# All four branch merges at the end of a layer, every gate in seven products

## The chip, the cores and the metric
The kernel runs on one core of a Trainium2 chip. Its time is device time in microseconds; of three runs the median is 1343.72 (1343.64 to 1344.62). A profile of one more execution shows what each engine did: TensorE (PE) multiplies matrices into PSUM, VectorE (DVE) and ScalarE (ACT) work element by element, GpSimd (POOL) raises a few numbers to a power, SyncE (SP) issues transfers.

## What is computed
A trunk of two layers on 512 tokens of width 1024, all in float32. A layer normalises its input, projects it with one wide matrix, runs four token mixers of width 512 (A, a gated linear recurrence; B, a state space model; C, an mLSTM; D, retention) and merges them:

```
hn = rmsnorm(x, norm_g);  proj = hn @ w_in          # 1024 x 12304: inputs of the mixers, then 4 x 1024 gates
y_a, y_b, y_c, y_d = ...                            # each 512 x 512, with its own output gate
up = einsum('bsnw,nwd->bsnd', [y_a, y_b, y_c, y_d], w_branch)
g = sigmoid(gates)                                  # 512 x 4 x 1024
x = x + sum_n(g * up) @ w_out
```

## The kernel before
Each float32 operand is split into a high and a low part, and a product is made of three matmuls, high by high, high by low and low by high (`mm3`, lines 330 to 333). The weights are in a list of pieces, `PLAN`, of 128 x 1024 numbers each, in the order of use. SP fetches them one after the other into three raw buffers (`wr`); ScalarE makes the high part (`wh`), VectorE the low one (`wl`), four buffers of each. Five pieces are asked for ahead of use.

TensorE follows the projections in the order in which `layer` calls them. `proj_T` and `proj_W` give outputs of 512 columns: 96 matmuls of 128x512 for a projection to 512 columns. In `proj_W` four accumulators of tokens (`pm`) are filled in turn, 6 matmuls each, over four pieces of weights.

A merge has four blocks of 256 gate columns. In merges A and B a block is a `proj_T` of the gates (48 matmuls of 512 columns) and one of the branch output (24). In merges C and D the gates of a block are computed by `seven`: gates and tokens are halved, rows of the weight too, and of the eight products of quarters seven are left, with sums of quarters as operands (Strassen's scheme in Winograd's form). It has 7 x 4 x 3 = 84 matmuls of 256 columns, and the same 24. The sums of activations (T1 to T4) are made once a layer by `combine`; T3 is written over a quarter of the normalised input by `in_place`, so that no projection can follow. The sums of weights are made for each block by `split7` on VectorE.

The mixers are generators (`branch_a` to `branch_d`, `finish_cd`) in a list of jobs. Behind pieces of a projection `pump(us)` hands the first job a credit of time, and the job puts its next instructions into the program until the credit is used up; the rate given to `start` scales it (a higher rate, more steps for the same credit). `drain` puts all that is left of a job there at once. A scheduler then orders each engine's instructions by priority; the evacuation of an accumulator and the weights go first. An engine runs its instructions in that order.

The order of a layer is: v of C, inputs of A and B, output gate of B, q and k of C, output gate of A; merge A; merge B, with C's mixer as a job at rate 0.4; q and k of D (one projection), v of D; o and z of C with D's mixer as a job and `combine` beside; z of D, with C's finish as a job; merge C, with D's finish; merge D; the output projection.

The lines that matter later: the splits of a branch output for a merge (yh, yl, lines 948 and 949), the rotary embedding of D's q and k (lines 1066 to 1070), C's exponents, scores and scaled keys (EC line 1255, PC line 1264, ke line 1270), B's last steps (xd, line 1238) with the transposes of `finish` (lines 401 and 860).

Of the kernel before, what the change touches and what calls it, by code (L numbers as in the profile page):

```python
# [10 lines left out]
AF = mybir.ActivationFunctionType  # L11
ALU = mybir.AluOpType
# [5 lines left out]
P = 128  # L18
NT = S // P
# [24 lines left out]

SEVEN = (2, 3)


def plan():  # L50
    u = []

    def proj(name, b, w=256):
        for h in range(2):
            u.append(("in", OFF[name] + 256 * b, h))

    def merge(n):
        for b in range(4):
            if n in SEVEN:
                for h in range(2):  # L60
                    u.append(("in7", OFF["g"] + 256 * (4 * n + b), h))
            else:
                proj("g", 4 * n + b)
            u.append(("br", n, 256 * b))

    def wide(*names):
        for name in names:
            for q in range(4):
                u.append(("in4", OFF[name], q))

    for name, b in BLOCKS:
        if b is None:
            wide(name)
        else:
            proj(name, b)
    merge(0)
    merge(1)

    wide("dq", "dv", "co", "cz", "dz")
    merge(2)  # L80
    merge(3)
    for q in range(4):
        u.append(("out4", 0, q))
    for b in range(2, 4):
        for h in range(2):
            u.append(("out", 256 * b, h))
    return u
# [10 lines left out]
D_DM, D_DS, D_COS, D_SIN, D_N = 0, 512, 768, 1024, 1280  # L98
# [6 lines left out]
def body(ctx, tc, x_in, wu, wz, ag, pp, br, fg, cst, cstd, out, xs, rows):  # L105
# [20 lines left out]
    def heap(name, shape=(P, 512), dt=F32):  # L126
        return hp.tile(list(shape), dt, name=nm(name), tag="h", bufs=NH)
# [4 lines left out]
    def tmain(name, shape=(P, 512), dt=F32):  # L132
        return hp.tile(list(shape), dt, name=nm(name), tag="tm", bufs=NTM)
# [186 lines left out]
    def drain(job):  # L320
        while any(j[0] is job for j in jobs):
            for _ in jobs[0][0]:
                pass
            jobs.pop(0)

    def start(job, rate):
        jobs.append((job, rate))
        return job
# [38 lines left out]
    def proj_W(acts, consume):  # L367

        ps = [psm() for _ in range(NT)]
        for q in range(4):  # L370
            hi, lo = take(1)[0]
            for t in range(NT):
                s = slice(t * P, (t + 1) * P)
                for i in range(2):
                    j = 2 * q + i
                    o = slice(512 * i, 512 * i + 512)
                    mm3(ps[t], acts[j][0][:, s], acts[j][1][:, s], hi[:, o], lo[:, o], j == 0, j == 7)
                if q == 3:
                    with tc.high_priority():
                        consume(t, ps[t])  # L380
                if t % 2:
                    pump(2.6)
# [39 lines left out]
    def gate2(dst, z):  # L422

        A.activation(dst, z, AF.Tanh, scale=0.5)
        V.scalar_tensor_tensor(dst, dst, 1.0, z, ALU.add, ALU.mult)
# [388 lines left out]
    def layer(l, hn, hn2, first=None):  # L814
        p, b = prm[l], brd[l]
# [83 lines left out]
        def quarter(r, s):  # L899
            return [[hn2[j][:, 4 * r + k, 256 * s:256 * s + 256] for k in range(4)] for j in range(2)]  # L900
# [30 lines left out]
        def in_place():  # L931
# [5 lines left out]
                    V.tensor_tensor(hn2[1][o], t3[kk], hn2[0].bitcast(F32)[o], ALU.subtract)  # L937
            bq["T3"] = quarter(0, 1)


        md = [None] * KT
        mp = [None] * KT

        def merge(n, y):
            yT = []
            for k in range(4):
                h, q = pair("y")
                A.copy(h, y[k])
                V.tensor_tensor(q, y[k], h.bitcast(F32), ALU.subtract)
                yT.append((h, q))  # L950
            tail = None
            if n == SEVEN[0]:
                in_place()
            for blk in range(4):
                th = [None, None]

                def use_g(ct, ps):
                    th[ct] = tmain("tg")
                    A.activation(th[ct], ps, AF.Tanh, scale=0.5)

                def use_up(ct, ps, blk=blk, th=th):
                    k = 2 * blk + ct
                    if n == 0:
                        md[k] = heap("md")
                        V.scalar_tensor_tensor(md[k], th[ct], 1.0, ps, ALU.add, ALU.mult)
                        return
                    V.scalar_tensor_tensor(th[ct], th[ct], 1.0, ps, ALU.add, ALU.mult)
                    V.tensor_tensor(md[k], md[k], th[ct], ALU.add)
                    if n == 3:
                        mp[k] = pair("mp")  # L970
                        A.activation(mp[k][0], md[k], AF.Copy, scale=0.5)
                        V.scalar_tensor_tensor(mp[k][1], md[k], 0.5, mp[k][0].bitcast(F32),
                                               ALU.mult, ALU.subtract)

                if n not in SEVEN:
                    proj_T(hn, use_g)
                    proj_T(yT, use_up, 1)
                    continue
                tail = seven(th, tail, yT, use_up)
            if n in SEVEN:  # L980
                tail()
# [4 lines left out]
        def seven(th, tail, yT, use_up):  # L986
# [58 lines left out]
                pump(2.6)  # L1045
            return rest

        merge(0, yA)

        drain(jB)  # L1050
        hC = []
        jC = start(branch_c(l, qT, kT, v1, am, fcs, em, hC), 0.4)

        merge(1, yB)


        qk = [None] * NT
        cos = cd[:, D_COS:D_COS + 256].rearrange("p (j t i) -> p j t i", j=2, t=NT)
        sin = cd[:, D_SIN:D_SIN + 256].rearrange("p (j t i) -> p j t i", j=2, t=NT)

        def use_qk(t, ps):

            r = heap("qk", [P, 8, 2, 32])
            u, v = tmain("ropeu", [P, 8, 2, 32]), tmain("ropev", [P, 8, 2, 32])
            for w, f in ((u, cos), (v, sin)):
                V.tensor_tensor(w.rearrange("p (j h) e i -> p j (h e) i", j=2),
                                ps.rearrange("p (j h i) -> p j h i", j=2, i=32),
                                f[:, :, t, :].unsqueeze(2).to_broadcast([P, 2, 8, 32]), ALU.mult)
            V.tensor_tensor(r[:, :, 0, :], u[:, :, 0, :], v[:, :, 1, :], ALU.subtract)
            V.tensor_tensor(r[:, :, 1, :], v[:, :, 0, :], u[:, :, 1, :], ALU.add)  # L1070
            qk[t] = r

        proj_W(hn, use_qk)
        vD = [heap("vD") for _ in range(NT)]
        proj_W(hn, lambda t, ps: A.copy(vD[t], ps))
        drain(jC)
        yDr = []
        jD = start(branch_d(qk, vD, yDr), 0.35)


        steps = combine()
        bq.update(B11=quarter(0, 0), B21=quarter(1, 0), B22=quarter(1, 1))
        tC = [heap("tC") for _ in range(NT)]

        def use_o(t, ps):
            A.activation(tC[t], ps, AF.Tanh, scale=0.5)
            V.scalar_tensor_tensor(hC[t], tC[t], 1.0, hC[t], ALU.add, ALU.mult)

        proj_W(hn, use_o)
        for _ in range(4):  # L1090
            next(steps, None)
        proj_W(hn, lambda t, ps: gate2(tC[t], ps))
        for _ in steps:
            pass

        def finish_cd(y, z, yT, mul, gcol):
            for j in range(4):
                yT[j] = heap("yC")
            for q in range(2):
                for t in (2 * q, 2 * q + 1):  # L1100
                    head_norm(y[t], z[t], mul)
                    yield 1.2
                if q:
                    for t in range(2):
                        finish(y[t], t, yT, gcol)
                    yield 2.4
            yield 1.2
            for t in range(2, NT):
                finish(y[t], t, yT, gcol)
            yield 2.4  # L1110

        drain(jD)
        yC = [None] * 4
        jF = start(finish_cd(hC, tC, yC, 0.25 / P, 44), 1.0)


        tD = [heap("tD") for _ in range(NT)]
        proj_W(hn, lambda t, ps: gate2(tD[t], ps))
        drain(jF)
        yD = [None] * 4  # L1120
        jG = start(finish_cd(yDr, tD, yD, 1.0 / P, 48), 0.5)
        merge(2, yC)
        drain(jG)
        merge(3, yD)
# [6 lines left out]
    def head_norm(y, z, mul):  # L1131

        sq = tran("sq")
        A.activation(sq, y, AF.Square)
        ss = small("hs", [P, 4])
        V.tensor_reduce(ss, sq.rearrange("p (h d) -> p h d", d=P), AX.X, ALU.add)
        r = small("hr", [P, 4])
        rsqrt(r, ss, mul, 4)
        y3 = y.rearrange("p (h d) -> p h d", d=P)
        V.tensor_tensor(y3, y3, bc(r, P), ALU.mult)  # L1140
        V.tensor_tensor(y, y, z, ALU.mult)
# [411 lines left out]
```

## Time and profile before
| | |
|---|---|
| median of three runs | 1343.72 us |
| profiled execution, its time | 1343.94 us |
| its span, first to last instruction | 1342.1 us |
| PE, DVE, ACT busy | 1327.7, 875.9, 578.5 us |
| merge A, B, C, D of layer 1 | 76.1, 80.9, 65.1, 63.4 us |
| granted TensorE clock, mean | 0.999 |

A row of the timeline gives an instruction's start and length in us. A matmul's end is modelled and overlaps the next one's start, so the distance of starts is its price, not its length. A row of the windows gives the length of a stage, and for each engine the busy time and number of instructions in it. A stage begins with its first projection matmul.

### The profile page before, as it was taken

How to read it: one execution, taken by the hardware profiler on the slowest of the kernel's cores; microseconds unless marked ns; L12 is line 12 of the kernel's file. 1: busy time of each engine (PE TensorE's matmuls, PEld its weight loads, DVE VectorE, ACT ScalarE, POOL GpSimd, SP SyncE). 2: the span in 40 equal slices, each digit the busy share in tenths (PEclk: the TensorE clock that was granted, in tenths of full speed). 3: DMA queues.
4: the chain of work that ended last, by engine and by line, in shares of the span. 5: the costliest groups of instructions: out<-in, count | busy, mean ns of one | idle time of the engine just before them, and what ended most of it. 6: DMA issues, size and time to landing. Idle time of an engine off the chain costs nothing.

```text
span 1342.1 us, 18162 instructions
## 1 busy us (share of the span) xinstructions
PE 1327.7 (99%) x7180; PEld 1123.7 (84%) x7180; DVE 875.9 (65%) x1504; ACT 578.5 (43%) x968; POOL 29.9 (2%) x53
## 2 busy tenths in 40 slices
PE   9999999999999999999999999999999999999998
PEld 8877888888888889998897778888888888899987
DVE  6668778444543798686466696873455448887845
ACT  6387334322213465454443963352222135554533
POOL 1000000000000020000000000000000000100000
PEclk9999999999999999999999999999999999999999
DMA  6223332333233223335332333333323322233351
GB/s 233 92 79 94 110 111 80 111 93 92 69 90 95 63 74 88 107 95 188 128 98 84 97 101 117 110 95 94 94 63 93 96 79 63 64 95 95 96 187 63
DMA packets 42181, 133.48 MB, mean 99 GB/s; under 512 B 5336, under 2 KB 5592, under 8 KB 42096
## 3 DMA queue, kind: packets, MB, share of 16 engines
q1 hardware_dynamic: 39504, 128.06, 30.9%
q10 hardware_dynamic: 2592, 4.27, 0.9%
q8 instruction: 56, 0.92, 0.3%
q14 instruction: 29, 0.24, 0.1%
HBM read 128.06 MB, written 4.24 MB: 99 GB/s over the span
## 4 chain that ended last, share of the span: by engine, by line
PE 84%; DVE 7%; ACT 6%; issue 2%; POOL 1%; DMA 0%; POOLq 0%; ACTq 0%; DVEq 0%
PE pm L331 23%; PE pm L332 23%; PE pm L333 23%; PE px L331 2%; PE px L333 2%; PE px L332 2%; PE px L1209 1%; ACT wh L278 1%; DVE wl L288 1%; PE pm L534 1%; PE px L401 1%; PE px L1282 1%; PE px L1262 1%; PE px L1362 1%; DVE cv L632 0%
## 5 line engine op out<-in xcount | busy, mean ns | idle before, releaser
L288 DVE TENSOR_TENSOR wl<-wr,wh 128x1024 fp32r<-128x1024 f32 (+1 forms) x184 | 225.1, 1224 | 240.3 <-ACT wh L278 239.4
L278 ACT CAST wh<-wr 128x1024 fp32r<-128x1024 f32 (+1 forms) x184 | 192.9, 1049 | 331.8 <-PE pm L332 170.1
L331 PE MATMUL pm<-hn,wh 128*128 128x512 f32 (+1 forms) x768 | 291.2, 379 | 0.0
L333 PE MATMUL pm<-hn,wl 128*128 128x512 f32 (+1 forms) x768 | 289.6, 377 | 0.0
L332 PE MATMUL pm<-hn,wh 128*128 128x512 f32 (+1 forms) x768 | 289.4, 377 | 0.0
L331 PE MATMUL pm<-wh,hn 128*128 128x512 f32 (+2 forms) x480 | 181.2, 378 | 1.3 <-DVE cv L632 1.3
L332 PE MATMUL pm<-wl,hn 128*128 128x512 f32 (+2 forms) x480 | 179.2, 373 | 0.0
L333 PE MATMUL pm<-wh,hn 128*128 128x512 f32 (+2 forms) x480 | 178.8, 373 | 0.0
L331 PEld LDWEIGHTS pm<-hn,wh 128*128 128x128 f32 x768 | 144.6, 188 | 30.3 <-issue 2.2
L332 PEld LDWEIGHTS pm<-hn,wh 128*128 128x128 f32 x768 | 144.5, 188 | 28.3 <-issue 0.4
L333 PEld LDWEIGHTS pm<-hn,wl 128*128 128x128 f32 x768 | 144.6, 188 | 27.8
L331 PEld LDWEIGHTS pm<-wh,hn 128*128 128x128 f32 x480 | 90.3, 188 | 19.5 <-ACT th L850 1.1
L333 PEld LDWEIGHTS pm<-wh,hn 128*128 128x128 f32 x480 | 90.3, 188 | 17.0
L332 PEld LDWEIGHTS pm<-wl,hn 128*128 128x128 f32 x480 | 90.4, 188 | 16.3 <-DVE wl L288 0.2
L331 PE MATMUL pm<-yh,wh 128*128 128x512 f32 x256 | 101.0, 397 | 0.0
L332 PE MATMUL pm<-yl,wh 128*128 128x512 f32 x256 | 100.7, 394 | 0.0
L333 PE MATMUL pm<-yh,wl 128*128 128x512 f32 x256 | 100.6, 394 | 0.0
L252 ACT CAST wh<-wr 128x1024 fp32r<-128x1024 f32 x48 | 50.4, 1050 | 54.1 <-DVE wr L263 43.6
L255 DVE TENSOR_TENSOR wl<-wr,wh 128x1024 fp32r<-128x1024 f32 x48 | 58.7, 1224 | 11.0 <-ACT wh L252 11.0
L332 PE MATMUL pm<-wl,mph 128*128 128x256 f32 (+1 forms) x192 | 61.4, 320 | 0.0
L331 PE MATMUL pm<-wh,mph 128*128 128x256 f32 (+1 forms) x192 | 61.3, 319 | 0.0
L333 PE MATMUL pm<-wh,mpl 128*128 128x256 f32 (+1 forms) x192 | 61.3, 319 | 0.0
(336 smaller groups left out, 2089.3 us busy)
## 6 DMA issues: line engine op xcount, KB each, us to landing
wr<-in_wu_dram SPq DMA_DIRECT2D x212, 512.0 KB, 3.6
row<-rows SPq DMA_DIRECT2D x24, 256.0 KB, 4.3
x<-in_x_dram SPq DMA_DIRECT2D x15, 256.0 KB, 5.3
wr<-in_wz_dram SPq DMA_DIRECT2D x4, 544.0 KB, 5.1
xs<-x ACTq DMA_DIRECT2D x8, 256.0 KB, 2.9
x<-xs SPq DMA_DIRECT2D x8, 256.0 KB, 6.4
out_dram<-xo SPq DMA_DIRECT2D x4, 256.0 KB, 2.1
out_dram<-xo ACTq DMA_DIRECT2D x4, 256.0 KB, 2.4
```

The source lines that it names most:

```text
L252: A.copy(w[0], s)
L255: V.tensor_tensor(w[1], s, w[0].bitcast(F32), ALU.subtract)
L278: h = A.copy(hi, raw)
L288: d = V.tensor_tensor(lo, raw, hi.bitcast(F32), ALU.subtract)
L331: mm(ps, lh, rh, start=first, stop=False, **kw)
L332: mm(ps, lh, rl, start=False, stop=False, **kw)
L333: lastpm[0] = mm(ps, ll, rh, start=False, stop=last, **kw)
L401: nc.tensor.transpose(ps[:, j * P:(j + 1) * P], src[:, j * P:(j + 1) * P], ident)
L534: pin(mm(bank[t][:, :272], xn[t, h][:, j * P:(j + 1) * P], ws.raw[h][:, 272 * j:272 * j + 272], start=h == 0 and j == 0, stop=h == 1 and j ...
L1209: mm(two(py, t)[:, 64 * e:64 * e + 64], M[e][:, t, :], xdt[t][:, o:o + 64], start=True, stop=True)
L1262: mm(ps[:, t], kT[h][:, s], qT[h][:, s], start=True, stop=True)
L1282: mm(pi[:, i], Ps[h][:, t], v1[t][:, h], start=True, stop=True)
```

## The change
All four gates are computed in seven products, and the four merges stand together at the end of the layer. q, k and v of D, o and z of C and z of D come ahead of merge A. C's mixer becomes a job before q and k of D, at rate 0.65 (was 0.4), behind what is left of B's mixer. The finishes of C and D both become jobs at the start of merge A, at rate 0.3 (were 1.0 and 0.5). The pieces of weights are listed in the new order; the projections, mixers and their numbers of instructions stay as they are.

```diff
-SEVEN = (2, 3)
+SEVEN = (0, 1, 2, 3)
...
-    merge(0)
-    merge(1)
 
     wide("dq", "dv", "co", "cz", "dz")
-    merge(2)
-    merge(3)
+    for n in range(4):
+        merge(n)
...
+        hC = []
+        jC = start(branch_c(l, qT, kT, v1, am, fcs, em, hC), 0.65)
...
+        proj_W(hn, use_qk)
+        vD = [heap("vD") for _ in range(NT)]
+        proj_W(hn, lambda t, ps: A.copy(vD[t], ps))
+        drain(jC)
+        yDr = []
+        jD = start(branch_d(qk, vD, yDr), 0.35)
...
+        proj_W(hn, use_o)
+        for _ in range(4):
+            next(steps, None)
+        proj_W(hn, lambda t, ps: gate2(tC[t], ps))
...
+        drain(jD)
...
+        tD = [heap("tD") for _ in range(NT)]
+        proj_W(hn, lambda t, ps: gate2(tD[t], ps))
...
+        yC, yD = [None] * 4, [None] * 4
+        jF = start(finish_cd(hC, tC, yC, 0.25 / P, 44), 0.3)
+        jG = start(finish_cd(yDr, tD, yD, 1.0 / P, 48), 0.3)
         merge(0, yA)
-
         drain(jB)
-        hC = []
-        jC = start(branch_c(l, qT, kT, v1, am, fcs, em, hC), 0.4)
-
         merge(1, yB)
...
         drain(jF)
-        yD = [None] * 4
-        jG = start(finish_cd(yDr, tD, yD, 1.0 / P, 48), 0.5)
         merge(2, yC)
         drain(jG)
         merge(3, yD)
```

On TensorE, in the projection to q and k of D, layer 1 (accumulators pm_3151 to pm_3154 before, pm_2086 to pm_2089 now; in the changed kernel the three matmuls of `mm3` are lines 329 to 331, the rotary embedding 951 to 955, C's mixer begins at 1250, the splits of y are at 1011), the order before held nothing else:

```order
L331 MATMUL pm_3153<-wh_3022,hn_120 128x512
L332 MATMUL pm_3153<-wl_3023,hn_120 128x512
L333 MATMUL pm_3153<-wh_3022,hn_121 128x512
L331 MATMUL pm_3153<-wh_3022,hn_120 128x512
L332 MATMUL pm_3153<-wl_3023,hn_120 128x512
L333 MATMUL pm_3153<-wh_3022,hn_121 128x512
L331 MATMUL pm_3154<-wh_3022,hn_120 128x512
```

In the changed kernel the same place has the last transposes of B's output (xd) and the first scores (qT, kT) and key transposes of C:

```order
L399 MATMUL px_2077<-cst_sb,xd_1590 128x128 x4
L399 MATMUL px_2120<-cst_sb,xd_1599 128x128 x4
L331 MATMUL pm_2088<-wh_1819,hn_121 128x512
L399 MATMUL px_2129<-cst_sb,xd_1608 128x128 x4
L1257 MATMUL px_2148<-qT_1387,kT_1543 128x128 x4
L1263 MATMUL px_2155<-cst_sb,kT_1543 128x128 x3
L329 MATMUL pm_2088<-wh_1819,hn_120 128x512
L330 MATMUL pm_2088<-wl_1820,hn_120 128x512
L331 MATMUL pm_2088<-wh_1819,hn_121 128x512
L329 MATMUL pm_2089<-wh_1819,hn_120 128x512
L330 MATMUL pm_2089<-wl_1820,hn_120 128x512
L331 MATMUL pm_2089<-wh_1819,hn_121 128x512
```

The last 60 small matmuls of B's mixer and the first 28 of C's now stand between the 96 of this projection; the 96 others of C's mixer stand in the projection to v of D behind it.

On VectorE, the rotary embedding of D's q and k (ropeu and ropev from the accumulators, then qk) stood before with only weight splits (wl) among it:

```order
L288 TENSOR_TENSOR wl_3218<-wr_3215,wh_3217 128x1024
L1066 TENSOR_TENSOR ropeu_3258<-pm_3151,cstd_sb 128x512
L1066 TENSOR_TENSOR ropev_3259<-pm_3151,cstd_sb 128x512
L1066 TENSOR_TENSOR ropeu_3271<-pm_3152,cstd_sb 128x512
L1066 TENSOR_TENSOR ropev_3272<-pm_3152,cstd_sb 128x512
L1066 TENSOR_TENSOR ropeu_3284<-pm_3153,cstd_sb 128x512
L1069 TENSOR_TENSOR qk_3257<-ropeu_3258,ropev_3259 128x8x32
L1069 TENSOR_TENSOR qk_3270<-ropeu_3271,ropev_3272 128x8x32
L1070 TENSOR_TENSOR qk_3257<-ropev_3259,ropeu_3258 128x8x32
L1070 TENSOR_TENSOR qk_3270<-ropev_3272,ropeu_3271 128x8x32
L288 TENSOR_TENSOR wl_3248<-wr_3245,wh_3247 128x1024
```

Now it has C's scores (PC), scaled keys (ke) and exponents (EC) among it:

```order
L954 TENSOR_TENSOR qk_2275<-ropeu_2276,ropev_2277 128x8x32
L954 TENSOR_TENSOR qk_2288<-ropeu_2289,ropev_2290 128x8x32
L955 TENSOR_TENSOR qk_2275<-ropev_2277,ropeu_2276 128x8x32
L951 TENSOR_TENSOR ropeu_2321<-pm_2088,cstd_sb 128x512
L951 TENSOR_TENSOR ropev_2322<-pm_2088,cstd_sb 128x512
L951 TENSOR_TENSOR ropeu_2334<-pm_2089,cstd_sb 128x512
L955 TENSOR_TENSOR qk_2288<-ropev_2290,ropeu_2289 128x8x32
L286 TENSOR_TENSOR wl_2266<-wr_2263,wh_2265 128x1024
L951 TENSOR_TENSOR ropev_2335<-pm_2089,cstd_sb 128x512
L1250 SCALAR_TENSOR_TENSOR EC_2295<-row_2247,am_646,cst_sb 128x128 x2
L1259 TENSOR_TENSOR PC_2306<-px_2301,EC_2295 128x512
L1265 TENSOR_TENSOR ke_2312<-px_2308,EC_2295 128x384
```

The product of the last scores, PC_2306, and ke_2312 stand behind all four accumulators' rotary products; C's first matmuls with v in the next projection need them.

On VectorE, at the start of merge D before (yl is the low part of a branch output, tg a half gate, md the merged sum, wal and wl weight splits of a block in seven products):

```order
L968 TENSOR_TENSOR md_2205<-md_2205,tg_4153 128x512
L949 TENSOR_TENSOR yl_4830<-yC_4168,yh_4829 128x512
L967 SCALAR_TENSOR_TENSOR tg_4154<-tg_4154,pm_4387 128x512
L255 TENSOR_TENSOR wal_4334<-wr_4280,wah_4333 128x512
L288 TENSOR_TENSOR wl_4150<-wr_4147,wh_4149 128x1024
L968 TENSOR_TENSOR md_2220<-md_2220,tg_4154 128x512
L1013 TENSOR_TENSOR tg_4353<-tg_4353,pm_4415 128x256
L949 TENSOR_TENSOR yl_4834<-yC_4169,yh_4833 128x512
L949 TENSOR_TENSOR yl_4838<-yC_4170,yh_4837 128x512
L949 TENSOR_TENSOR yl_4842<-yC_4171,yh_4841 128x512
```

And at the start of merge B now:

```order
L1011 TENSOR_TENSOR yl_3964<-yB_1962,yh_3963 128x512
L253 TENSOR_TENSOR wal_3988<-wr_3903,wah_3987 128x512
L1011 TENSOR_TENSOR yl_3968<-yB_1963,yh_3967 128x512
L1011 TENSOR_TENSOR yl_3972<-yB_1964,yh_3971 128x512
L1011 TENSOR_TENSOR yl_3976<-yB_1965,yh_3975 128x512
L1075 TENSOR_TENSOR tg_4007<-tg_4007,pm_4054 128x256
L1011 TENSOR_TENSOR yl_4626<-yC_3244,yh_4625 128x512
L1011 TENSOR_TENSOR yl_4630<-yC_3245,yh_4629 128x512
L1081 TENSOR_TENSOR tg_4008<-tg_4008,px_4009 128x256
L1011 TENSOR_TENSOR yl_4634<-yC_3246,yh_4633 128x512
L253 TENSOR_TENSOR wl_3982<-wr_3979,wh_3981 128x1024
L1011 TENSOR_TENSOR yl_4638<-yC_3247,yh_4637 128x512
```

Behind B's four splits those of C's output follow in the same block, and further on those of D's; before, each merge had its own four at its start.

## Rows read from the trace of the kernel before
**Rows 1.** The page: busy time by engine; chain of waits by engine.
```profile
PE 1327.7 (99%) x7180; PEld 1123.7 (84%) x7180; DVE 875.9 (65%) x1504; ACT 578.5 (43%) x968; POOL 29.9 (2%) x53
...
PE 84%; DVE 7%; ACT 6%; issue 2%; POOL 1%; DMA 0%; POOLq 0%; ACTq 0%; DVEq 0%
```

**Rows 2.** What PE waited for, first two of six: us in total, times, longest.
```profile
PE px L401 <- DVE xn L450: 2.1, 4, 0.6
PE px L401 <- DVE xd L1238: 1.7, 4, 0.6
```

**Rows 3.** Windows of layer 1: length; busy us (count) of PE, PEld, DVE, ACT, POOL; clock; DMA.
```profile
136.00:158.40 22.40, 22.40 (x97) 18.02 (x96) 20.85 (x28) 7.40 (x10) 0.00 (x0) 1.00 0.26 76
213.80:289.90 76.10, 75.24 (x349) 61.38 (x348) 38.17 (x72) 28.50 (x54) 2.59 (x4) 1.00 0.34 104
289.90:370.80 80.90, 80.90 (x414) 68.03 (x413) 43.52 (x77) 19.83 (x27) 0.00 (x0) 1.00 0.26 79
370.80:393.10 22.30, 22.30 (x98) 18.09 (x97) 9.29 (x12) 4.14 (x4) 0.00 (x0) 1.00 0.33 94
...
...
497.60:562.70 65.10, 64.89 (x450) 59.88 (x449) 51.76 (x74) 35.73 (x70) 0.00 (x0) 1.00 0.30 85
562.70:626.10 63.40, 63.33 (x433) 58.16 (x432) 47.13 (x67) 29.86 (x49) 0.00 (x0) 1.00 0.40 122
```

**Rows 4.** Windows of merges A to D, layer 2, same columns.
```profile
877.60:953.80 76.20, 75.36 (x350) 61.47 (x350) 38.16 (x72) 28.52 (x54) 2.58 (x4) 1.00 0.34 104
953.80:1034.60 80.80, 80.80 (x413) 67.99 (x412) 43.52 (x77) 19.72 (x26) 0.00 (x0) 1.00 0.27 79
1161.50:1227.30 65.80, 64.97 (x449) 59.94 (x448) 52.48 (x75) 35.65 (x69) 0.00 (x0) 1.00 0.30 89
1227.30:1290.80 63.50, 63.41 (x434) 58.10 (x433) 47.27 (x67) 29.98 (x50) 0.00 (x0) 1.00 0.40 122
```

**Rows 5.** Timeline of PE in merge D: start, length, instruction.
```profile
608.68 0.28 PE L332 MATMUL px<-hn,wah 128*128 128x256 f32 x1
608.80 0.28 PE L333 MATMUL px<-hn,wal 128*128 128x256 f32 x1
608.92 0.39 PE L331 MATMUL pm<-yh,wh 128*128 128x512 f32 x1
609.15 0.39 PE L332 MATMUL pm<-yl,wh 128*128 128x512 f32 x1
```

**Rows 6.** Timeline of DVE, merge A's surroundings and the rotary embedding.
```profile
203.78 1.23 DVE L288 TENSOR_TENSOR wl<-wr,wh 128x1024 fp32r<-128x1024 f32 x1
204.92 1.65 DVE L1185 TENSOR_SCALAR E<-row,am 128x128 f32<-128x128 f32 x8
...
230.32 1.13 DVE L1255 SCALAR_TENSOR_TENSOR EC<-row,am,cst_sb 128x128 f32<-128x128 f32 x4
...
389.92 0.68 DVE L1066 TENSOR_TENSOR ropeu<-pm,cstd_sb 128x512 f32<-128x512 f32 x1
390.52 0.68 DVE L1066 TENSOR_TENSOR ropev<-pm,cstd_sb 128x512 f32<-128x512 f32 x1
...
392.91 0.75 DVE L1069 TENSOR_TENSOR qk<-ropeu,ropev 128x256 f32<-128x256 f32 x2
```

**Rows 7.** Lines of DVE in merge B and after: count, busy us, mean ns.
```profile
L1264 DVE TENSOR_TENSOR PC<-px,EC 128x512 f32<-128x512 f32 x4 | 2.7, 687 | 6.0 <-PE px L1262 6.0
...
L949 DVE TENSOR_TENSOR yl<-yB,yh 128x512 fp32r<-128x512 f32 x4 | 2.5, 684 | 0.0
...
L1270 DVE TENSOR_TENSOR ke<-px,EC 128x384 f32<-128x384 f32 x4 | 2.2, 546 | 0.0
```

**Rows 8.** Timeline of ACT at the start of merge A.
```profile
228.10 2.42 ACT L860 ACTIVATE yB<-px,half 128x128 f32<-128x128 f32 x8
...
232.40 0.61 ACT L948 CAST yh<-yA 128x512 fp32r<-128x512 f32 x1
```

**Rows 9.** The page: weight loads of one line, count, busy us, mean ns.
```profile
L331 PEld LDWEIGHTS pm<-hn,wh 128*128 128x128 f32 x768 | 144.6, 188 | 30.3 <-issue 2.2
```

More of the change, by code (lines that the diff above doesn't have):

```diff
@@ L938, in in_place, with use_qk, use_o, finish_cd @@
             bq["T3"] = quarter(0, 1)
+        hC = []
+        jC = start(branch_c(l, qT, kT, v1, am, fcs, em, hC), 0.65)
+        qk = [None] * NT
+        cos = cd[:, D_COS:D_COS + 256].rearrange("p (j t i) -> p j t i", j=2, t=NT)
+        sin = cd[:, D_SIN:D_SIN + 256].rearrange("p (j t i) -> p j t i", j=2, t=NT)
+        def use_qk(t, ps):
+            r = heap("qk", [P, 8, 2, 32])
+            u, v = tmain("ropeu", [P, 8, 2, 32]), tmain("ropev", [P, 8, 2, 32])
+            for w, f in ((u, cos), (v, sin)):
+                V.tensor_tensor(w.rearrange("p (j h) e i -> p j (h e) i", j=2),
+                                ps.rearrange("p (j h i) -> p j h i", j=2, i=32),
+                                f[:, :, t, :].unsqueeze(2).to_broadcast([P, 2, 8, 32]), ALU.mult)
+            V.tensor_tensor(r[:, :, 0, :], u[:, :, 0, :], v[:, :, 1, :], ALU.subtract)
+            V.tensor_tensor(r[:, :, 1, :], v[:, :, 0, :], u[:, :, 1, :], ALU.add)
+            qk[t] = r
+        proj_W(hn, use_qk)
[4 more added lines that the diff above has]
+        jD = start(branch_d(qk, vD, yDr), 0.35)
+        steps = combine()
+        bq.update(B11=quarter(0, 0), B21=quarter(1, 0), B22=quarter(1, 1))
+        tC = [heap("tC") for _ in range(NT)]
+        def use_o(t, ps):
+            A.activation(tC[t], ps, AF.Tanh, scale=0.5)
+            V.scalar_tensor_tensor(hC[t], tC[t], 1.0, hC[t], ALU.add, ALU.mult)
+        proj_W(hn, use_o)
+        for _ in range(4):
+            next(steps, None)
+        proj_W(hn, lambda t, ps: gate2(tC[t], ps))
+        for _ in steps:
+            pass
+        def finish_cd(y, z, yT, mul, gcol):
+            for j in range(4):
+                yT[j] = heap("yC")
+            for q in range(2):
+                for t in (2 * q, 2 * q + 1):
+                    head_norm(y[t], z[t], mul)
+                    yield 1.2
+                if q:
+                    for t in range(2):
+                        finish(y[t], t, yT, gcol)
+                    yield 2.4
+            yield 1.2
+            for t in range(2, NT):
+                finish(y[t], t, yT, gcol)
+            yield 2.4
+        drain(jD)
+        tD = [heap("tD") for _ in range(NT)]
+        proj_W(hn, lambda t, ps: gate2(tD[t], ps))
         md = [None] * KT
@@ L1046, in seven @@
             return rest
+        yC, yD = [None] * 4, [None] * 4
+        jF = start(finish_cd(hC, tC, yC, 0.25 / P, 44), 0.3)
+        jG = start(finish_cd(yDr, tD, yD, 1.0 / P, 48), 0.3)
         merge(0, yA)
         drain(jB)
-        hC = []
-        jC = start(branch_c(l, qT, kT, v1, am, fcs, em, hC), 0.4)
         merge(1, yB)
-        qk = [None] * NT
-        cos = cd[:, D_COS:D_COS + 256].rearrange("p (j t i) -> p j t i", j=2, t=NT)
-        sin = cd[:, D_SIN:D_SIN + 256].rearrange("p (j t i) -> p j t i", j=2, t=NT)
@@ L1061, in use_qk @@
[L1061 to L1118, printed above, removed]
         drain(jF)
-        yD = [None] * 4
-        jG = start(finish_cd(yDr, tD, yD, 1.0 / P, 48), 0.5)
         merge(2, yC)
```

## Prediction
> **What bounds the kernel now.** I read the page's sums first, then what the matrix engine waits for, then stage by stage busy times, then single starts in the timeline. The sums say that TensorE is busy 99% of the span and holds 84% of the chain that ended last, against 65% for VectorE and 43% for ScalarE [rows 1]. It hardly waits: there are six kinds of wait, of which the two longest add up to 2.1 and 1.7 us [rows 2], and none is on C's mixer. So a stage lasts as long as the matmuls issued in it, and the question is what their number and size do to it.
>
> The stages give the price of a matmul. The q projection of C is 96 matmuls of 512 columns with nothing beside them and takes 22.40 us [rows 3], so one costs 0.2333 us. A merge that isn't done in seven products has 288 of these, 67.2 us; merge A lasted 76.1 us and merge B 80.9 us [rows 3]. The rest, 8.9 and 13.7 us, is for 60 small matmuls of B's mixer and 124 of C's that are issued there (110 ns each for C's). A merge in seven products, merge D, has nothing beside it and lasted 63.4 us, 63.5 in layer 2 [rows 3, 4]; it has 336 matmuls of 256 columns and 96 of 512. In its timeline the small ones start 0.12 us apart, the large ones 0.23 [rows 5]: half the columns, half the time.
>
> **The change part by part.** Gates of A and B: each block of 256 gate columns loses 48 large matmuls (11.2 us) and gains 84 small ones (10.1 us at 0.12). I take the whole merge as measured, with its small waits inside: 67.2 us becomes 63.4, twice in a layer, 7.6 us; in layer 2, with 63.5, 7.4 us. Together 15.0 us.
>
> The Trainium skill speaks against this step: "TensorE: Matmul & The Clock Gate", section "Back-to-back issue gap", gives for sustained pairs of weight load and matmul about 81 ns at 128 columns and 131 ns at 512. An estimate of mine on the line between these two figures is 98 ns at 256, by which a block would pay 84 x 98 = 8.2 us in place of 48 x 131 = 6.3 us and the change would lose some 31 us over 16 blocks. The rows measure 120 and 233 ns, so the measurement decides for the gain.
>
> Moves on TensorE: the order of the changed kernel has every small matmul of the mixers still once. B's last 60 and C's first 28 now stand in D's q and k, C's other 96 in D's v, and the 32 transposes that finish C and D move from the z projection of D and merge C into merges A and B; sixteen of them made merge C 65.1 us long, 1.7 more than merge D [rows 3]. TensorE pays the same for them wherever they stand, so I cost the moves at nothing there. The weights come in equal pieces and number, and the 63.4 us contain their flow at a DMA share of 0.40 [rows 3]; C's four row loads move on SP's queue from among merge B's weights to among those of D's v, three buffers ahead of use as before.
>
> What can cost is VectorE. Beside D's q and k it had 9.29 us of work in 22.3 us [rows 3]. Now it first has to end B's mixer, which after the start of merge A took it 16.5 us (213.8 to 230.32, where C's first exponent is formed [rows 6]). Behind it the order has, up to the last product of C's scores: 16 exponent pieces (four in 1.13 us), 4 score products and 4 scalings (687 and 546 ns), 8 rotary products, 8 half-width sums, 3 weight splits. By the starts (0.28, 0.60, 0.46, 0.60, 0.33 and 1.14 us [rows 6, 7]) that is 4.5 + 2.4 + 1.8 + 4.8 + 2.6 + 3.4 = 19.5 us, so VectorE is through 36.0 us after the stage began. TensorE needs 22.3 + 8.9 + 28 x 0.110 = 34.3 us for the stage and then has 18 large matmuls and 5 small ones of D's v, 4.7 us, before it asks for that product: 3.0 us of cover. Against it stands one wait: C's first score product needs an exponential which ScalarE has behind 12 copies of B's output (eight took 2.42 us, so 3.6 us, and 0.6 us for itself [rows 8]); that gives 4.2 - 3.0 = 1.2 us if VectorE idles all that time, nothing if it doesn't. What would be late next is the rotary part, whose accumulators D's v writes again, one every 6 matmuls, 1.4 us.
>
> The Trainium skill has a rule here too: "VectorE: DVE Perf Modes", section "The DRAIN you can't avoid", says that the next operation doesn't start until the pipe is empty. By it whole durations would count. The rows show the next start 0.08 us before the recorded end, and 0.09 in the longer ones [rows 6].
>
> If whole durations counted, these 43 operations would take 0.08 us more each, 3.4 us, and the wait would be 4.6. So the cost lies between 0 and 4.6 us in a layer; I take 1.0, near the sum by starts, because starts are what the rows show.
>
> A second place is the start of merge B. Eleven splits of y (684 ns on VectorE [rows 7], 0.61 on ScalarE [rows 8]), B's four, C's four and three of D's, now stand in the order close together. A block of merge D needs 47.13 / 4 = 11.8 us of VectorE in 15.85 [rows 3]; with 11 x 0.60 = 6.6 us it would be 18.4, 2.6 too many. But the order spreads them over more than a block and a half, and C's and D's fill places in which the weights of a next block can't be split yet. Bounds 0 and 2.6 us a layer, taken as 0. At the start of merge A the splits and the in-place write of T3 are those which merge C had, and with them it lasted 65.1 us.
>
> Sum, against the profiled execution's own 1343.94 us (1342.1 of span and 1.8 around it): -15.0 + 2 x 1.0 = -13.0, 1330.9 us. The median of the runs is 0.2 us under that execution, so 1330.7.
>
> **The rivals.** (1) VectorE is late in D's q and k by the full 4.6 us a layer: 1330.7 + 2 x 3.6 = 1337.9. For it speaks that it would be the fullest stage of the layer; against it that its work there still is only about as long as TensorE's. The rule of the drain leads here too.
> (2) That, and the pile at merge B holds up the weights by its full 2.6 us a layer: 1337.9 + 5.2 = 1343.1, no change. Against the second half: merge D comes after merge C's end with four splits of its own and lasts only 0.7 us more than its starts alone give (4 x 15.68 = 62.7).
> (3) Slower: C's mixer becomes a chain that TensorE follows. Beside D's q, k and v its steps stand 9 to 24 large matmuls apart, where in merge B they stood 24 or 36 apart, and each goes TensorE, VectorE, ScalarE, VectorE, TensorE. In merge B VectorE was busy 43.52 us, of which 12 x 1.14 + 16 x 0.60 = 23.3 is the merge's own, so C's part is about 20 us a layer. All of it waited for gives 1330.7 - 2.0 + 40 = 1368.7. It decides from 7.5 us of waits a layer, where the gain is gone. Against it: TensorE showed no wait on it in merge B, and even 9 matmuls are 2.1 us, enough for two or three operations of a step.
> (4) Seven products don't pay because each small matmul waits for its weight load: at 188 ns a load [rows 9] a block takes 84 x 0.188 + 24 x 0.233 = 21.4 us in place of 16.8, 74 us over 16 blocks, 1417. The starts 0.12 us apart all but rule it out. The first rule cited above ends on this side as well, at 1343.7 + 31 = 1375 by its own figures, and shares this chance.
>
> **How the numbers follow.** My forecast has 0.81, with 1325 to 1335 as its own range: the low end is no wait at VectorE (1328.7), blocks at the starts' price (15.68 in place of 15.85 us, 2.7 less) and the 1.7 us of waits of B's last transposes [rows 2] gone too, about half of it; the high end is half of rival 1. Rival 1 has 0.09, 2 has 0.05, 3 has 0.04, 4 has 0.01. A measurement of this kernel tells about 0.2%, 2.7 us, from no change. Faster by more: the forecast and rival 1, 0.90. Within: rival 2, 0.05. Slower: rivals 3 and 4, 0.05. The range that should hold 8 in 10 is 1325 to 1338, with rival 1 in it.
>
> **What would show it.** Right: merges A and B last 63 to 64 us plus 4 us of transposes between them; D's q and k about 34 to 36 us; D's v 32 to 33 (22.3 + 96 x 0.110); the z projection of D 22.4. Wrong in the first step: a merge with nothing beside it that lasts over 65 us. Wrong in the second: TensorE waits on VectorE's score products or rotary operations in D's q, k and v of over 2 us a layer. Wrong in the third: waits on weight splits in merge B's first two blocks. The forecast as a whole is wrong if the time is over 1341 us.

## The result and the profile after

The changed kernel takes 1328.23 us (median of four runs, 1327.89 to 1328.90) against 1344.03 us of the kernel before in the same comparison: a ratio of 0.9883, with a 95% interval of 0.9866 to 0.9900. That is 15.8 us less; the forecast was 13.0 less, with 1330.7 us. The profiled execution took 1328.9 us, its span is 1327.0 us, and the granted clock is 0.999 as before.

The page's sums and the chain by engine of the changed kernel stand against [rows 1]:

```profile
PE 1311.7 (99%) x7756; PEld 1140.6 (86%) x7756; DVE 962.0 (72%) x1648; ACT 619.1 (47%) x1064; POOL 34.4 (3%) x53
...
PE 76%; DVE 11%; ACT 7%; issue 3%; DMA 2%; POOL 1%; POOLq 0%; ACTq 0%; DVEq 0%
```

TensorE has 576 more matmuls (four merges with 4 x 36 more each) and is busy 16.0 us less; it is still busy 99% of the span. VectorE has 86 us more work, nearly all of it brought by the seven products of A and B, and its share of the chain rose from 7 to 11%.

Stage by stage, the windows of layer 1 (columns as in [rows 3]): D's q and k, D's v, z of D, then merges A, B, C and D.

```profile
214.10:250.60 36.50, 35.54 (x201) 30.22 (x200) 28.41 (x66) 13.15 (x32) 3.05 (x4) 1.00 0.30 101
250.60:282.00 31.40, 31.40 (x178) 26.94 (x177) 22.02 (x54) 7.25 (x10) 0.00 (x0) 1.00 0.21 68
339.50:361.80 22.30, 22.30 (x98) 18.08 (x97) 21.56 (x38) 11.02 (x16) 6.05 (x6) 1.00 0.21 64
361.80:428.40 66.60, 65.81 (x457) 60.67 (x456) 48.30 (x70) 35.74 (x73) 4.06 (x2) 1.00 0.26 83
428.40:492.70 64.30, 64.11 (x442) 59.11 (x441) 51.90 (x74) 35.31 (x65) 0.00 (x0) 1.00 0.31 99
492.70:555.80 63.10, 63.10 (x434) 58.24 (x433) 47.24 (x66) 27.23 (x45) 0.00 (x0) 1.00 0.32 101
555.80:619.20 63.40, 63.21 (x433) 58.12 (x432) 47.09 (x67) 29.94 (x49) 0.00 (x0) 1.00 0.38 121
```

Against [rows 3], merge A went from 76.1 to 66.6, B from 80.9 to 64.3, C from 65.1 to 63.1; D stayed at 63.4. D's q and k took up 14.2 us and D's v 9.1 us. Layer 2 repeats this (A 66.4, B 64.4, C 63.1, D 63.5).

C's scores and the rotary embedding aren't among TensorE's waits in the changed kernel. The longest wait in the merges is that of the first matmul of a product for the addition `tg`. It isn't new. The first line is of the kernel before, where the addition is line 1013 and only merges C and D have it; the second is of the changed kernel, line 1075 (us in total, times, longest):

```profile
PE pm L331 <- DVE tg L1013: 1.0, 3, 0.7
...
PE pm L329 <- DVE tg L1075: 1.7, 3, 0.8
```

This is how it looks in the timeline of the changed kernel, in the first block of merge A (start, length, instruction, idle time before it and releaser):

```profile
363.74 1.22 DVE L286 TENSOR_TENSOR wl<-wr,wh 128x1024 fp32r<-128x1024 f32 x1
363.98 3.06 POOL L393 TENSOR_TENSOR hr<-hr,mhalf 128x4 f32<-128x4 f32 x1 [4.99 <-DVE hr L392]
...
365.48 0.68 DVE L1011 TENSOR_TENSOR yl<-yA,yh 128x512 fp32r<-128x512 f32 x1
...
367.06 0.69 DVE L1135 TENSOR_TENSOR yD<-yD,hr 128x512 f32<-128x512 f32 x1 [0.90 <-POOL hr L393]
367.07 0.28 PE L330 MATMUL px<-hn,wh 128*128 128x256 f32 x1
367.67 0.41 DVE L1075 TENSOR_TENSOR tg<-tg,pm 128x256 f32<-128x256 f32 x1
...
368.14 0.38 PE L329 MATMUL pm<-T,wh 128*128 128x256 f32 x1 [0.80 <-DVE tg L1075]
```

VectorE stands still for 0.90 us, because the head norm of D needs `hr` from GpSimd. Behind that norm on VectorE's queue is `tg`, which empties the product A12 out of its accumulator `pm`. The product S1 is written into the other half of the same accumulator, so its first matmul starts 1.07 us after its predecessor instead of 0.12.

### The profile page after: what moved, and what is told of

It reads as the page before. It is cut to its first block, busy times and chain, and to the rows that moved or that the text cites. A ratio compares the mean times of both kernels' runs of the same rounds, so it can differ in the third digit from the quotient of the medians.

```text
span 1327.0 us, 19610 instructions
## 1 busy us (share of the span) xinstructions
PE 1311.7 (99%) x7756; PEld 1140.6 (86%) x7756; DVE 962.0 (72%) x1648; ACT 619.1 (47%) x1064; POOL 34.4 (3%) x53
## 4 chain that ended last, share of the span: by engine, by line
PE 76%; DVE 11%; ACT 7%; issue 3%; DMA 2%; POOL 1%; POOLq 0%; ACTq 0%; DVEq 0%
PE pm L329 20%; PE pm L330 19%; PE pm L331 19%; PE px L329 3%; PE px L330 3%; PE px L331 3%; DVE wl L253 2%; DMA wr<-in_wu_dram 1%; ACT wh L250 1%; ACT wh L276 1%; PE px L1204 1%; DVE wl L286 1%; PE px L399 1%; DVE tg L1029 1%; POOL hr L393 1%
## 5 line engine op out<-in xcount | busy, mean ns | idle before, releaser
L286 DVE TENSOR_TENSOR wl<-wr,wh 128x1024 fp32r<-128x1024 f32 (+1 forms) x152 | 185.9, 1224 | 111.0 <-ACT wh L276 110.4
L276 ACT CAST wh<-wr 128x1024 fp32r<-128x1024 f32 (+1 forms) x152 | 159.4, 1049 | 208.2 <-PE pm L331 106.1
L329 PE MATMUL pm<-hn,wh 128*128 128x512 f32 (+1 forms) x640 | 225.0, 352 | 0.0
L331 PE MATMUL pm<-hn,wl 128*128 128x512 f32 (+1 forms) x640 | 224.3, 351 | 0.0
L330 PE MATMUL pm<-hn,wh 128*128 128x512 f32 (+1 forms) x640 | 224.3, 350 | 0.0
L250 ACT CAST wh<-wr 128x1024 fp32r<-128x1024 f32 x96 | 100.5, 1051 | 85.6 <-DVE wr L261 76.6
L329 PEld LDWEIGHTS pm<-hn,wh 128*128 128x128 f32 x640 | 120.5, 188 | 20.1 <-issue 2.2
L330 PEld LDWEIGHTS pm<-hn,wh 128*128 128x128 f32 x640 | 120.5, 188 | 18.2 <-issue 0.4
L253 DVE TENSOR_TENSOR wl<-wr,wh 128x1024 fp32r<-128x1024 f32 x96 | 117.3, 1223 | 25.3 <-ACT wh L250 25.2
L331 PEld LDWEIGHTS pm<-hn,wl 128*128 128x128 f32 x640 | 120.5, 188 | 16.6
L329 PE MATMUL px<-T,wh 128*128 128x256 f32 x256 | 72.5, 283 | 0.0
L330 PE MATMUL px<-T,wh 128*128 128x256 f32 x256 | 71.9, 281 | 0.0
L331 PE MATMUL px<-T,wl 128*128 128x256 f32 x256 | 71.8, 280 | 0.0
```

Of the source, the lines that this page charges most:

```text
L250: A.copy(w[0], s)
L253: V.tensor_tensor(w[1], s, w[0].bitcast(F32), ALU.subtract)
L276: h = A.copy(hi, raw)
L286: d = V.tensor_tensor(lo, raw, hi.bitcast(F32), ALU.subtract)
L329: mm(ps, lh, rh, start=first, stop=False, **kw)
L330: mm(ps, lh, rl, start=False, stop=False, **kw)
```

## The experiments

**Order alone.** `SEVEN = (0, 1, 2, 3)` becomes `SEVEN = (2, 3)` in the changed kernel.

> The changed kernel with the gates of A and B back in eight products: the new order alone. Theory 1 (the gain is the seven products, 15 us, and the order is worth nothing): 1343 to 1345 us; merges A and B without their transposes last 67 to 68 us again and D's q and k keep their 36.6 us. Rival (the order gives part of the gain, because the mixers' matmuls fall into fewer visits and the z projection of D is free of transposes): 1341 or less. Second rival (the order costs time that the products' gain hid): over 1346.

1341.09 us (1340.83 to 1341.36), ratio 0.9980 (0.9971 to 0.9989). So the order gives 2.7 us of the gain and the seven products of A and B give 12.9; the number is nearest to the first rival's (1341 or less). In its windows merges A and B of layer 1 have no product in seven, but 288 large matmuls each, with 24 and 8 small ones of the finishes among them:

```profile
361.20:430.70 69.50, 69.50 (x314) 56.70 (x313) 25.82 (x30) 25.91 (x50) 0.00 (x0) 1.00 0.33 99
430.70:498.50 67.80, 67.80 (x298) 55.02 (x297) 37.10 (x46) 27.15 (x44) 0.00 (x0) 1.00 0.28 86
```

Set against the changed kernel's 66.6 and 64.3 the seven products save 2.9 and 3.5 us; in layer 2 (69.6 and 67.7 against 66.4 and 64.4) 3.2 and 3.3. Together 12.9, the whole difference of the times.

**VectorE's rotary products twice.** In `use_qk`:

```diff
-            for w, f in ((u, cos), (v, sin)):
+            for w, f in ((u, cos), (v, sin), (u, cos), (v, sin)):
```

> The 8 rotary products of D's q and k are each computed twice, 8 x 0.60 = 4.8 us more of VectorE a layer in the stage that I took for its fullest; the result is the same. Theory 1 (the cover there is used up: in the changed kernel's trace VectorE ends C's last scaled keys at 256.2 us and TensorE asks for them at 256.25): TensorE waits for most of it, 3 to 4.8 us a layer, 1334 to 1338. Rival (TensorE has other matmuls to do, the scheduler puts C's last products behind them, and only the accumulators of D's v wait): under 1.5 us a layer, below 1331.5.

1328.75 us (1328.26 to 1330.36), ratio 0.9891 (0.9876 to 0.9906): no change. D's q, k and D's v in its windows:

```profile
213.90:250.70 36.80, 35.74 (x202) 30.09 (x200) 28.60 (x65) 13.22 (x33) 3.07 (x4) 1.00 0.30 101
250.70:282.10 31.40, 31.40 (x176) 27.02 (x177) 26.15 (x63) 7.28 (x10) 0.00 (x0) 1.00 0.21 68
```

Most of VectorE's added 4.8 us appears in D's v (22.02 to 26.15 us), and the two stages are longer by 0.3 and 0.0 us. In this kernel's order the scheduler had moved C's last products with v from 18 to 36 large matmuls into D's v. VectorE's lateness is therefore no cost in this stage, and a fixed number of large matmuls as cover was the wrong picture: the scheduler sets the cover anew when the work grows.

**C's mixer slower.** Its rate 0.65 becomes 0.4.

> The changed kernel with C's mixer issued at a rate of 0.4 in place of 0.65, so that the last head's scores stand 36 large matmuls into D's v, and the products of the last two groups of heads come at or behind the last large matmul of D's v. Theory (the third rival of the prediction is real but lies at the end of C's mixer: as long as 12 or more large matmuls, 2.8 us, stand between two steps they are free, and a step with none between is paid whole): each of the two or three steps behind the last large matmul is paid with its chain of VectorE and ScalarE, 2 to 4 us a step, 4 to 10 us a layer, 1336 to 1348. Other theory (the order of D's output gate moves up beside them, or VectorE is through long before): under 1 us a layer, 1327 to 1330.

1326.69 us (1326.07 to 1327.14), ratio 0.9871 (0.9856 to 0.9886). The stage o of C in its windows:

```profile
277.60:308.80 31.20, 31.20 (x188) 25.84 (x186) 18.95 (x45) 8.82 (x24) 0.00 (x0) 1.00 0.21 68
```

My expectation of 4 to 10 us a layer fails. The last steps do stand behind D's v, but not bare: in its order they lie between the first ten large matmuls of o of C, which don't need them, and TensorE is busy all of the 31.2 us. C's chain (the third rival) doesn't hold TensorE up here. The kernel is even 1.5 us faster than the changed one, less than two comparisons can tell apart, but its windows say where: merge A has 1.1 and 0.9 us less, because the head norm now stands behind `tg`, and the wait for `tg` is 0.2 us in all instead of 1.7. So the gain is that of the next experiments.

**Finishes later.** The two `start(finish_cd(...))` lines stand behind merge A, with rate 0.45.

> The finishes of C and D start behind merge A instead of at its start, at rate 0.45. Theory 1 (the 0.95 us that TensorE waits in merge A's first block in each layer, for the evacuation of the product A12, is VectorE's pile of head norms in front of it): those waits go, about 2 us off, 1326. Rival (the wait is that of the first block itself, whose weight splits and T3 come late, whatever the jobs do): within 0.7 us of 1328.2.

1328.87 us (1328.49 to 1329.23), ratio 0.9889 (0.9876 to 0.9903): no change. Merges A and B in its windows, and its wait for `tg`:

```profile
361.20:425.40 64.20, 63.26 (x434) 58.10 (x433) 48.30 (x70) 29.68 (x50) 4.06 (x2) 1.00 0.28 87
425.40:492.20 66.80, 66.52 (x465) 61.63 (x464) 52.34 (x74) 41.46 (x89) 0.00 (x0) 1.00 0.31 95
...
PE pm L329 <- DVE tg L1075: 2.6, 6, 0.8
```

All 24 transposes have left merge A, and it is shorter by just their 2.4 us (66.6 to 64.2), still 1.8 us over the 62.4 of the next experiment. So the finishes' matmuls aren't what it waits for. But the head norms stay where they were on VectorE, because the scheduler places them ahead of the job's place in the program: in the first block of merge A VectorE still stands still for 0.90 us at one of them, and TensorE for 0.79 us behind `tg`. What theory 1 was about was left in place, so this experiment doesn't decide between it and the rival.

**Two accumulators.** In `seven`, A12 and S1 no longer share one accumulator:

```diff
-            Y = psm([P, 2, 256])
-            product(Y[:, 0], "A12", "B21", True)
+            Y0 = psm([P, 256])
+            product(Y0, "A12", "B21", True)
...
-            product(Y[:, 1], "S1", "T1", True)
+            Y = psm([P, 256])
+            product(Y, "S1", "T1", True)
```

> The products A12 and S1 of a block get an accumulator each in place of the two halves of one. Theory 1 (S1 clears the bank that A12's sum is still read from, so each block waits 0.08 to 0.95 us for VectorE there and restarts 0.1 us late): 16 blocks a layer lose 0.2 us less each and merge A's first block 0.9, together 6 to 8 us off, 1320 to 1322. Rival (the wait moves to the next accumulator, since the four are now all in use): within 1 us of 1328.2.

1319.47 us (1319.16 to 1320.65), ratio 0.9821 (0.9808 to 0.9835), 8.8 us less than the changed kernel. Its merges A to D of layer 1:

```profile
361.50:426.70 65.20, 65.20 (x458) 60.41 (x457) 47.87 (x70) 35.71 (x73) 4.43 (x2) 1.00 0.27 85
426.70:490.20 63.50, 63.49 (x442) 58.92 (x441) 52.11 (x74) 35.46 (x65) 0.00 (x0) 1.00 0.33 102
490.20:552.60 62.40, 62.40 (x434) 57.94 (x433) 47.22 (x66) 27.19 (x45) 0.00 (x0) 1.00 0.33 102
552.60:614.80 62.20, 62.20 (x434) 57.87 (x432) 47.08 (x67) 30.09 (x49) 0.00 (x0) 1.00 0.39 123
```

Now a merge with nothing beside it lasts 62.2 to 62.4 us, which is what the starts of [rows 5] give (336 x 0.12 + 96 x 0.233 = 62.7, with 0.12 rounded up). The same place in merge A, in this kernel's timeline:

```profile
363.68 3.06 POOL L393 TENSOR_TENSOR hr<-hr,mhalf 128x4 f32<-128x4 f32 x1 [4.99 <-DVE hr L392]
...
366.77 0.69 DVE L1136 TENSOR_TENSOR yD<-yD,hr 128x512 f32<-128x512 f32 x1 [0.90 <-POOL hr L393]
366.86 0.28 PE L331 MATMUL pm<-T,wl 128*128 128x256 f32 x1
...
366.98 0.28 PE L329 MATMUL pm<-T,wh 128*128 128x256 f32 x1
...
367.38 0.41 DVE L1075 TENSOR_TENSOR tg<-tg,pm 128x256 f32<-128x256 f32 x1
```

VectorE is exactly as late as before, and `tg` too. TensorE is already in S1 when `tg` starts, with its matmuls 0.12 us apart. It was the shared accumulator that handed VectorE's delay on.

The first block is the worst, but not the only one. Over the 16 blocks of layer 1 of the changed kernel the first matmul of S1 starts 0.12 to 1.07 us behind the one before it, and in 15 of them the next follows after 0.22 or 0.23 us, where 0.12 would do for both. That is 4.2 us in the layer and, doubled, 8.4 of the 8.8 us. With two accumulators all these distances are 0.11 to 0.13 us. The runs don't tell whether the memory asks for this wait or only the program, which allocates the two halves as one buffer: every experiment with this edit gives S1 a buffer of its own.

**The same edit on the kernel before.** There merges C and D alone are in seven products (the expectation's first sentence is tangled; this is what it means).

> The kernel before, where merges A and B are in 12 small and 96 large... that is, not in seven products, and C and D are; changed only in that the seven products' A12 and S1 have separate accumulators in place of the two halves of one. Theory (the wait for A12's evacuation before S1, and the restart behind it, is paid in each block in seven products, whatever else the order does): merges C and D lose their excess over the starts' price of 1.11, 1.08, 1.89 and 1.12 us, so about half of the 8.8 us that the same edit saved in the changed kernel, 1339 to 1340 us. By it the change is worth more with this edit on both sides: about 20 us (1339.5 - 1319.5) in place of 15.8. Rival (the shared accumulator costs only in the new order, where merges follow each other without a break): no change, 1343 to 1344.

1338.63 us (1338.26 to 1339.05), ratio 0.9960 (0.9947 to 0.9972): 5.5 us less, a little more than the 4 to 5 expected. Merges C and D, 65.1 and 63.4 us in [rows 3], in its windows:

```profile
497.30:561.30 64.00, 64.00 (x450) 59.69 (x449) 51.83 (x74) 35.66 (x70) 0.00 (x0) 1.00 0.30 87
561.30:623.60 62.30, 62.30 (x433) 57.95 (x432) 47.16 (x67) 30.06 (x49) 0.00 (x0) 1.00 0.42 125
```

So each merge in seven products pays for the shared accumulator, before the change as after it. With two accumulators on both sides the change is worth about 19 us (1338.63 - 1319.47 = 19.2, from two comparisons).

**A sum behind the power.** GpSimd's `hr` takes 1.01 us in 14 of its 16 places in the changed kernel and 3.06 in two. Beside the one at 357.98, for instance, VectorE ran its sum of squares, with one input (357.75 to 358.43); at 363.98 splits with two inputs followed without a break until 366.16, and `hr` ended 0.88 us after them. The experiment puts a sum there in all places:

```diff
         rsqrt(r, ss, mul, 4)
+        s2 = small("hs2", [P, 4])
+        V.tensor_reduce(s2, sq.rearrange("p (h d) -> p h d", d=P), AX.X, ALU.add)
```

> The changed kernel with one more VectorE operation in each of the 16 head norms of C and D, straight behind the operation that GpSimd's power (hr) waits for: a second sum over the same squares, 0.6 us by starts, whose result nobody uses. Where it stood in the changed kernel hr took 1.01 us in 14 of its 16 places and 3.06 us in two, once a layer at the start of merge A, and VectorE then stood still for 0.90 us with the evacuation of A12 queued behind, so that TensorE's fifth product waited 0.95 us. Theory (hr can't read beside VectorE's operations with two inputs in SBUF, and in these two places alone such operations followed it without a break): with an operation of one input behind it hr takes 1.0 us in all 16 places, VectorE's pause at the start of merge A goes, and merge A loses about 0.8 us in either layer, 1326 to 1327.5. Rival (these two places are slow for a reason that lies in GpSimd or in its semaphores): 3.06 us stays in them, and the time is that of the changed kernel, 1328 to 1329, or some tenths more for the added work.

1328.16 us (1327.87 to 1328.38), ratio 0.9882 (0.9866 to 0.9899). The theory on `hr` holds, the price doesn't. `hr` takes 1.01 us in 14 places and 1.31 in the two others, where the scheduler put a split (`yl`) between. In this kernel's timeline:

```profile
369.24 0.69 DVE L1011 TENSOR_TENSOR yl<-yA,yh 128x512 fp32r<-128x512 f32 x1
369.47 1.31 POOL L393 TENSOR_TENSOR hr<-hr,mhalf 128x4 f32<-128x4 f32 x1 [6.89 <-DVE hr L392]
```

It ends at 370.78, 0.85 us after the split. The Trainium skill, "SBUF — State Buffer", section "Who interferes with whom", says that a VectorE instruction with two inputs in SBUF contends with a GpSimd instruction that reads SBUF. The 0.85 us agree with it for an `hr` that comes while such a VectorE operation runs. Where `hr` starts first, the changed kernel shows no contention: there `hr` takes 1.01 us, and a split with two inputs that starts 0.07 us behind it takes 1.23, the usual time.

```profile
371.64 1.01 POOL L393 TENSOR_TENSOR hr<-hr,mhalf 128x4 f32<-128x4 f32 x1 [4.61 <-DVE hr L392]
...
371.71 1.23 DVE L253 TENSOR_TENSOR wl<-wr,wh 128x1024 fp32r<-128x1024 f32 x1 [0.21 <-ACT wh L250]
```

But merge A of the experiment lasts 66.6 us, as in the changed kernel. In the other order that the added sums made, ScalarE evacuates the first product late, behind a weight cast, and TensorE waits for that:

```profile
363.13 1.03 ACT L276 CAST wh<-wr 128x1024 fp32r<-128x1024 f32 x1
363.31 0.28 PE L330 MATMUL pm<-hn,wh 128*128 128x256 f32 x1
364.06 0.37 ACT L1066 COPY tg<-px 128x256 f32<-128x256 f32 x1
364.49 0.38 PE L329 MATMUL px<-T,wh 128*128 128x256 f32 x1 [0.90 <-ACT tg L1066]
```

One wait took the other's place, 1.18 us from start to start.

**Best version: two accumulators, B's end later.** Beside the two accumulators, B's two last yields are 8.0 in place of 5.0, and C's rate is 0.9.

> The kernel with separate accumulators, and with the weights of B's two last yields raised from 5.0 to 8.0, so that the third and fourth group of B's closing transposes come 60 instead of 38 and 39 large matmuls into D's q and k, and C's mixer at a rate of 0.9 in place of 0.65, so that it still ends before D's v does. Theory (of the 2.2 us that D's q and k last longer than their matmuls' price, 0.70 and 0.66 us are these transposes waiting for VectorE's normalised xd): 1.0 to 1.4 us a layer less, 1317 to 1318. Rival (the wait moves to C's steps, which now follow each other closer): no change or slower, 1319 to 1322.

1317.87 us (1317.33 to 1318.46), ratio 0.9805 (0.9792 to 0.9819), the lowest median of all. D's q, k and D's v in its windows:

```profile
213.20:247.70 34.50, 33.97 (x189) 28.95 (x188) 26.89 (x63) 14.06 (x33) 3.06 (x4) 1.00 0.35 107
247.70:280.30 32.60, 32.60 (x191) 28.31 (x190) 22.82 (x57) 6.33 (x10) 0.00 (x0) 1.00 0.20 65
```

The two stages together last 67.1 us instead of the 67.9 that they last in the changed kernel and with two accumulators alone, and TensorE waits for `xd` twice (1.1 us in all) instead of four times (1.9). That is 0.8 us a layer, 1.6 in all, a little less than the expected 1.0 to 1.4 a layer. The two edits, of B's yields and of C's rate, were made together, and no run tells them apart.

## Why the prediction came out as it did

**Seven products in A and B: right in mechanism, 15.0 us forecast, 12.9 measured.** The price of 63.4 us for a merge was read from merge D [rows 3], small waits included. Merge B pays that: 64.3 us less 8 transposes of 0.1 us is 63.5. Merge A doesn't: 66.6 less 24 of them (2.4) is 64.2. Of the 2.1 us that are missing, 1.4 are in the two merges A. The step that missed is "I take the whole merge as measured, with its small waits inside": the waits depend on what VectorE has at that place, and the first block of A comes when the head norm of D is on its queue. I had read merge D's small waits as part of the price and not asked whose they were, though the trace of the kernel before named one: TensorE waiting for `tg`, 1.0 us in three times. The two-accumulator kernel shows that they were a shared accumulator's, 0.7 to 1.4 us of each merge in seven products, and that without them a merge costs 62.4.

Weight loads don't bound the small matmuls (the fourth rival): 62.4 us is the 0.12 us of [rows 5] kept through 336 of them. The figures of the Trainium skill, "TensorE: Matmul & The Clock Gate", section "Back-to-back issue gap", by which the prediction worked out 1375 us, aren't those of this stage.

**Moves on TensorE: forecast 0, measured 2.7 us of gain for the order as a whole.** The step that failed is "TensorE pays the same for them wherever they stand". By the stages' sums this is 0.8 us in layer 1 and 1.6 in layer 2. Merge C is 0.4 and 1.1 of it: it lasted 65.1 and 65.8 us with its 16 transposes and lasts 63.1 without them, and they cost 1.6 us, 0.1 each, where they are now. In layer 1 the z projection of D is another 0.8: it lasted 24.7 us with its 16 transposes and lasts 22.3. The rest, some of it losses, is spread over several stages, and no run isolates it. I also counted wrongly, ahead of the prediction too: D's q and k hold 44 small matmuls of C's, not 28, and D's v 80, not 96. These lines of the changed kernel in that stage show it:

```profile
L1257 PE MATMUL px<-qT,kT 128*128 128x128 f32 x32 | 4.2, 274 | 0.0
...
L1263 PE MATMUL px<-cst_sb,kT 128*128 128x128 f32 x12 | 2.0, 273 | 0.0
```

With 16 more at 0.11 us the forecast for D's q and k is 36.1 instead of 34.3, against 36.5 measured, and D's v 31.1 instead of 32.9, against 31.4. The sum of both was right.

**VectorE in D's q and k: forecast 2.0 us, measured none.** TensorE waits on no score product and no rotary operation, and 4.8 us of added rotary work cost nothing. The step that failed is the fixed cover of 18 large matmuls, with VectorE's sum of starts set against it. By the sum VectorE would be through 36.0 us after the stage began and TensorE would ask 3.0 us later. In the changed kernel VectorE is through with the last `ke` at 256.22, 42.1 us after the beginning: it stood still before three of the four score products, for 1.70, 2.83 and 0.80 us, more than the one wait that I had counted. But TensorE asks for that `ke` only at 256.25, 0.03 us later, because its stage was longer and it had other matmuls to do:

```profile
243.79 0.69 DVE L1259 TENSOR_TENSOR PC<-px,EC 128x512 f32<-128x512 f32 x1 [2.83 <-PE px L1257]
...
255.06 0.69 DVE L1259 TENSOR_TENSOR PC<-px,EC 128x512 f32<-128x512 f32 x1 [0.80 <-ACT EC L1253]
255.67 0.55 DVE L1265 TENSOR_TENSOR ke<-px,EC 128x384 f32<-128x384 f32 x1
...
256.25 0.61 PE L1293 MATMUL px<-v,ke 128*128 128x129 f32 x4
```

So the cover was used up and still nothing was lost; with the rotary products twice the scheduler moved the point where TensorE asks. What the stage does lose, some 1.4 us, are the closing transposes of B waiting for `xd`, a wait that merge A had already [rows 2]:

```profile
229.26 0.39 PE L330 MATMUL pm<-wl,hn 128*128 128x512 f32 x1
230.20 1.19 PE L399 MATMUL px<-cst_sb,xd 128*128 128x128 f32 x8 [0.54 <-DVE xd L1233]
231.14 0.47 PE L331 MATMUL pm<-wh,hn 128*128 128x512 f32 x1
232.03 0.52 PE L399 MATMUL px<-cst_sb,xd 128*128 128x128 f32 x3 [0.42 <-DVE xd L1233]
```

The starts are 0.94 and 0.89 us apart where 0.233 would do.

**Pile of splits at merge B: forecast 0, right.** Merge B has no wait on a weight split. What I should have looked at is not the weights' splits but the evacuations queued among them.

**The rivals.** C's chain (the third) didn't appear even at the lower rate. The first two begin with VectorE late in D's q and k, and TensorE lost nothing there. The forecast was 2.5 us too slow (1330.7 against 1328.23). By the experiments 2.7 of the order and 2.0 of VectorE were missed on one side and 2.1 of the products on the other, 2.6 in all: that the size came out near is partly luck, because the misses had different signs.

## What to carry to other kernels

When a measured stage is used as a price, take it apart first: starts times count, and then each wait in it with its owner, because the waits don't move with the work. Where two results shared one accumulator in this kernel, the second didn't start until the first was emptied, so that a delay on the emptying engine became TensorE's; another accumulator was worth 8.8 us, more than half of what the whole change brought. And where a scheduler places the work, cover isn't a constant: doubling work on an engine with slack cost nothing here, and neither did delaying a chain.

## What the runs showed of the hardware

A matmul of 256 columns that starts behind a wait is followed after 0.22 us instead of 0.12 (368.14 to 368.36 in the changed kernel, and the same in 14 other blocks of the layer), so a wait costs about 0.1 us more than itself. Coming back from small matmuls to the large ones costs about as much, 0.32 us in place of 0.23 to the next start (0.31 to 0.34 at 21 places between 200 and 700 us):

```profile
243.76 0.48 PE L329 MATMUL pm<-wh,hn 128*128 128x512 f32 x1
244.08 0.39 PE L330 MATMUL pm<-wl,hn 128*128 128x512 f32 x1
244.31 0.39 PE L331 MATMUL pm<-wh,hn 128*128 128x512 f32 x1
```

By these starts many short visits to a mixer would cost more than few long ones, by some 0.09 us a visit; that is an estimate, and no experiment isolated it. And a power of 128 x 4 numbers on GpSimd took 1.01 us, or 3.06 us where VectorE was in a row of operations with two inputs, without a break, when it started; one that started ahead of such an operation took 1.01 us beside it.
